# Output stage of a hybrid decoder layer: the samples' product with the weights as the stationary operand

## Chip, cores and metric

The kernel runs on one NeuronCore of a Trainium2 chip. A time is that of one execution on the device, in microseconds. The kernel before was run three times and its median is quoted; one more execution was recorded by the profiler, and all rows come from that one.

## What is computed

One inference step of one decoder layer, for a prompt of 512 positions and for 8 sample sequences of 4 positions each (32 rows). Three token mixers (mLSTM, chunked spatial gating, RG-LRU) share one input projection; their outputs are gated, projected and merged. The change touches only the end:

```python
merged = (jax.nn.sigmoid(g_a) * (y_a @ p['w_proj_a'])
          + jax.nn.sigmoid(g_b) * (y_b @ p['w_proj_b'])
          + jax.nn.sigmoid(g_c) * (y_c @ p['w_proj_c']))
out = merged @ p['w_out']                                    # 1024 x 1024
x_new = layer_norm(ALPHA * x + out, p['ln_g'], p['ln_b'])
```

`x_new` is an output for the prompt's 512 rows (`y_p`) and for the samples' 32 rows (`y_s`), all in float32.

## The kernel before

A matmul on TensorE loads one operand (the stationary one, at most 128x128) and moves the columns of the other past it. Products are made to nearly float32 precision from two parts: each operand is split into a high part (rounded to the type that TensorE multiplies, float32r) and a low part (the rest), and high x high, low x high and high x low are added up in PSUM. The low part's name ends in `l`, the high part's in `h`.

All engines but SyncE run their instructions in the order in which the program writes them. SyncE's DMA issues are ordered by the framework.

`output()` (line 1223) is the last stage. The merged activations lie transposed, features on the partitions: `ms[k]` (k = 0 to 7) is a pair of high and low parts, 128 features x 544 positions, the last 32 of them the samples. `msx` holds the samples alone, for each k 32 high columns and 32 low ones beside each other. The output weights come in two halves of 512 columns; `wos[hf, k]` is the pair of parts of 128 rows x 512 columns. While the first half (`hf` 0) is multiplied, the second half's weights are loaded and split (`wout_half`).

In each half the rows are done in five pieces: four tiles of 128 prompt rows (`i` = 0 to 3) and the samples (`i` = `NCH` = 4). In half 0 the samples come last, in half 1 first (`orders`), so the samples' two products follow each other. A prompt tile takes 24 matmuls: the activations are stationary (128x128), 512 weight columns move. The samples take 16 in each half: 64 columns of `msx` are stationary against the high weights, and 32 against the low ones. The result of the samples' matmuls has high and low rows on different partitions (0 to 31 and 32 to 63), so it is evacuated by VectorE (line 1277), then by ScalarE (line 1283), and added by VectorE (line 1284).

After each piece VectorE adds half of PSUM to the residual `r[i, hf]` (line 1277) and takes the statistics of two times 256 columns (`bn_stats`). In half 1 the norm follows for each piece, here called its finish: `ln_stats` (VectorE, with a reciprocal root on GpSimd, line 1151), half 0's columns on VectorE (`ln_out`, lines 1155 and 1156), half 1's columns on ScalarE and GpSimd (lines 1325 and 1326), an add of VectorE that is put off to the next piece's finish (`late`, line 1331), and two DMAs to the output. The last tile is multiplied in two parts of 256 columns. `rows_in` loads a residual tile and scales it on ScalarE (lines 1244 and 1245), some pieces ahead. PSUM tiles of the kind `aux` (one bank, two buffers) hold the results here; those of the kind `mm` (two banks, two buffers) are the input projections'.

Of the kernel before, what the change touches and what calls it, by code (L numbers as in the profile page):

```python
# [15 lines left out]
P = 128  # L16
D = 1024
KT = 8
# [23 lines left out]
def kernel(  # L42
# [22 lines left out]
    def mm(name):  # L65
        return pm.tile([P, 2, 512], F32, tag="mm", name=name)
# [26 lines left out]
    def matmul(out, a, b, start, stop):  # L93
        cols = math.prod(b.shape[1:])
        clk[0] += cols / 2400 if b.dtype == F32R and cols >= 256 else max(cols, 16) / 600
        PE.matmul(out, a, b, start=start, stop=stop)  # L96
# [1049 lines left out]
    def ln_stats(stt, n, name):  # L1146
        ag = sp.tile([P, 2], F32, tag="bag", name=f"bag{name}", bufs=2)
        V.bn_aggr(ag[:n], stt[:n])
        rs = sp.tile([P, 1], F32, tag="brs", name=f"brs{name}", bufs=2)
        V.tensor_scalar(rs[:n], ag[:n, 1:2], EPS, None, op0=ALU.add)  # L1150
        G.tensor_tensor(rs[:n], rs[:n], mhalf[:n], op=ALU.pow)
        return ag, rs

    def ln_out(out, src, ag, rs, g, b, n):
        V.scalar_tensor_tensor(out, src, ag[:n, 0:1], g[:n, :512], op0=ALU.subtract, op1=ALU.mult)
        V.scalar_tensor_tensor(out, out, rs[:n], b[:n, :512], op0=ALU.mult, op1=ALU.add)
# [66 lines left out]
    def output():  # L1223
        force("wout")
        for c in range(KT - 2, KT):
            ms.append(split(f"ms{c}", mg[c][:, :T], ("x", "x")))

        msx = slot("dm", "msx", F32R)[:, :512].rearrange("p (k c) -> p k c", k=KT)
        for c in range(KT):
            for i in range(2):  # L1230
                G.tensor_copy(msx[:, c, i * NS:(i + 1) * NS], f(ms[c][i][:, SEQ:T]))
        orders = ((0, 1, 2, 3, NCH), (NCH, 0, 1, 2, 3))
        r, stts, late = {}, {}, []
        og, ob = [], []
        nxt = None
        every = [(hf, i) for hf in range(2) for i in orders[hf]]

        def rows_in():
            if len(r) < len(every):
                hf, i = every[len(r)]  # L1240
                n = P if i < NCH else NS
                t_ = slot("dm" if len(r) == 8 else "ya", f"r{i}{hf}")
                src = xpv[i * P:i * P + n] if i < NCH else xsv
                nc.sync.dma_start(t_[:n, :512], src[:, hf * 512:hf * 512 + 512])
                A.activation(t_[:n, :512], t_[:n, :512], AF.Copy, scale=ALPHA)
                r[i, hf] = t_

        rows_in()
        for hf in range(2):
            if hf == 1:  # L1250
                for q in range(2):
                    for dst, src in ((og, ln_g), (ob, ln_b)):
                        a = slot("kv", f"ol{len(dst)}{q}")
                        nc.sync.dma_start(a[:, :512], src[0:1, q * 512:q * 512 + 512].to_broadcast([P, 512]))
                        dst.append(a)
            for oi, i in enumerate(orders[hf]):
                n = P if i < NCH else NS
                rows_ = slice(i * P, i * P + n)
                dst = y_p[0, rows_] if i < NCH else y_s.rearrange("b s d -> (b s) d")
                t_ = r[i, hf]  # L1260

                last = hf == 1 and oi == NCH
                for c0 in range(0, 512, 256) if last else (0,):
                    cw = slice(c0, c0 + 256) if last else slice(0, 512)
                    ps = aux(f"out{i}{hf}{c0}")[:, cw]
                    for k in range(KT):
                        wh_, wl_ = (w_[:, cw] for w_ in wos[hf, k])
                        if i < NCH:
                            for n_, (a, b) in enumerate(((ms[k][0], wh_), (ms[k][1], wh_), (ms[k][0], wl_))):
                                matmul(ps, a[:, rows_], b, start=(k == 0 and n_ == 0), stop=(k == KT - 1 and n_ == 2))  # L1270
                        else:
                            if k:
                                matmul(ps[:NS, :], msx[:, k, 0:NS], wl_, start=False, stop=False)
                            matmul(ps[:2 * NS, :], msx[:, k, :], wh_, start=(k == 0), stop=(k == KT - 1))
                            if k == 0:
                                matmul(ps[:NS, :], msx[:, k, 0:NS], wl_, start=False, stop=False)
                    V.scalar_tensor_tensor(t_[:n, cw], ps[:n, :], 0.5, t_[:n, cw], op0=ALU.mult, op1=ALU.add)
                    if last:
                        V.bn_stats(stts[i][:n, 2 + c0 // 256, :], t_[:n, cw])
                rows_in()  # L1280
                if i == NCH:
                    lo = sp.tile([P, 512], F32, tag="c0l", name=f"outl{hf}", bufs=2)
                    A.activation(lo[:NS, :], ps[NS:2 * NS, :], AF.Copy, scale=0.5)
                    V.tensor_tensor(t_[:NS, :512], t_[:NS, :512], lo[:NS, :], op=ALU.add)
                if hf == 0:
                    for k in (2 * oi, 2 * oi + 1):
                        if k < KT:
                            raw, hi, lo = wout_half(1, k)
                            A.activation(hi[:, :512], raw, AF.Copy)
                            V.tensor_tensor(lo[:, :512], raw, f(hi[:, :512]), op=ALU.subtract)  # L1290
                            wos[1, k] = (hi[:, :512], lo[:, :512])
                    stts[i] = sp.tile([P, 4, 6], F32, tag="bsto", name=f"bsto{i}", bufs=5)
                if not last:
                    for q in range(2):
                        V.bn_stats(stts[i][:n, 2 * hf + q, :], t_[:n, q * 256:q * 256 + 256])
                if hf == 0:
                    continue
                ag, rs = ln_stats(stts[i], n, f"o{i}")
                if not last:
                    for fin in late:  # L1300
                        fin()
                    late.clear()
                t_, ra = r[i, 1][:n, :512], r[i, 0][:n, :512]
                if last:

                    qa, qb = slice(0, 384), slice(384, 512)
                    parts = ((ra, og[0][:n, :512], ob[0][:n, :512]), (t_[:, qa], og[1][:n, qa], ob[1][:n, qa]))
                    for x_, g_, _ in parts:
                        V.scalar_tensor_tensor(x_, x_, ag[:n, 0:1], g_, op0=ALU.subtract, op1=ALU.mult)
                    nm = sp.tile([P, 1], F32, tag="bnm", name=f"bnm{i}", bufs=2)  # L1310
                    V.scalar_tensor_tensor(nm[:n], ag[:n, 0:1], -1.0, rs[:n], op0=ALU.mult, op1=ALU.mult)
                    A.activation(t_[:, qb], t_[:, qb], AF.Identity, bias=nm[:n], scale=rs[:n])
                    G.tensor_tensor(t_[:, qb], t_[:, qb], og[1][:n, qb], op=ALU.mult)
                    G.tensor_tensor(t_[:, qb], t_[:, qb], ob[1][:n, qb], op=ALU.add)
                    for x_, _, b_ in parts:
                        V.scalar_tensor_tensor(x_, x_, rs[:n], b_, op0=ALU.mult, op1=ALU.add)
                        c0 = 0 if x_ is ra else 512
                        nc.sync.dma_start(dst[:, c0:c0 + x_.shape[-1]], x_)
                    for fin in late:
                        fin()  # L1320
                    nc.sync.dma_start(dst[:, 896:1024], t_[:, qb])
                    continue
                nm = sp.tile([P, 1], F32, tag="bnm", name=f"bnm{i}", bufs=2)
                V.scalar_tensor_tensor(nm[:n], ag[:n, 0:1], -1.0, rs[:n], op0=ALU.mult, op1=ALU.mult)
                A.activation(t_, t_, AF.Identity, bias=nm[:n], scale=rs[:n])
                G.tensor_tensor(t_, t_, og[1][:n, :512], op=ALU.mult)
                ln_out(r[i, 0][:n, :512], r[i, 0][:n, :512], ag, rs, og[0], ob[0], n)
                nc.sync.dma_start(dst[:, 0:512], r[i, 0][:n, :512])

                def fin(t_=t_, dst=dst, n=n):  # L1330
                    V.tensor_tensor(t_, t_, ob[1][:n, :512], op=ALU.add)
                    nc.sync.dma_start(dst[:, 512:1024], t_)

                late.append(fin)


    for h in range(H):
# [52 lines left out]
```

## Time and profile before

| | |
|---|---|
| median of 3 runs | 990.83 us (989.39 to 991.03) |
| the profiled execution | 991.64 us |
| its span on the core | 989.9 us |
| TensorE busy | 975.1 us (99% of the span), 7427 matmuls |
| VectorE, ScalarE, GpSimd busy | 56%, 42%, 10% |
| granted TensorE clock, mean | 0.988 of full speed |

The span runs from the first to the last instruction of the core; the execution's time holds 1.7 us more around it. Busy TensorE time counts matmuls that overlap each other in the array, so a matmul's duration is longer than the step from one to the next; steps are read from starts.

### The profile page before, as it was taken

To read this page: it belongs to the slowest core of one execution; us is meant where nothing else is said; L and a number is where in the kernel's file an instruction comes from. 1 tells how busy PE (TensorE), PEld (TensorE's weight loads), DVE (VectorE), ACT (ScalarE), POOL (GpSimd) and SP (SyncE) were. 2 spreads that over 40 slices of the span, in tenths; PEclk is the share of its full clock that TensorE was granted. 3 is DMA by queue.
4 is the path that set the end of the run, shared out by engine and by line. 5 is a ranking of instruction groups with operands and counts; after the bars stand their busy time and mean duration, and the time that the engine had idled before them with its cause. 6 is when DMAs were issued, how large, how long until landed. Compare 5 with 4: busy or idle time off the path is not lost.

```text
span 989.9 us, 17773 instructions
## 1 busy us (share of the span) xinstructions
PE 975.1 (99%) x7427; PEld 950.7 (96%) x7427; DVE 549.6 (56%) x892; ACT 411.2 (42%) x648; POOL 97.3 (10%) x218
## 2 busy tenths in 40 slices
PE   8999999999999999999999999999999999999996
PEld 7999999999999999999999999999999999999975
DVE  3565676566567568889942243333257555433456
ACT  3455446445444544889922232222232313322421
POOL 5121101200210120001000000000000000000204
PEclk7999999999999999999999999999999999999998
DMA  6342723541362253332132222232222313431322
GB/s 209 106 99 91 214 71 98 170 132 62 116 215 67 81 183 95 97 96 92 57 115 85 86 86 85 88 109 90 85 86 96 102 54 107 138 107 44 102 64 101
DMA packets 99392, 103.55 MB, mean 105 GB/s; under 512 B 5342, under 2 KB 91720, under 8 KB 99312
## 3 DMA queue, kind: packets, MB, share of 16 engines
q1 hardware_dynamic: 98416, 102.11, 33.0%
q8 instruction: 58, 0.95, 0.4%
q0 software_dynamic: 896, 0.31, 0.1%
q14 instruction: 22, 0.18, 0.1%
HBM read 90.40 MB, written 12.00 MB: 103 GB/s over the span
## 4 chain that ended last, share of the span: by engine, by line
PE 98%; DMA 1%; ACT 0%; issue 0%; POOL 0%; SPq 0%; DVE 0%; POOLq 0%
PE ps_v L96 5%; PE out L96 5%; PE ps_zc L96 5%; PE ps_u L96 5%; PE ps_z L96 5%; PE ps_q L96 5%; PE ps_vb L96 5%; PE ps_xc L96 5%; PE ps_pa L96 5%; PE ps_zb L96 5%; PE ps_ga L96 5%; PE ps_pc L96 5%; PE ps_o L96 5%; PE ps_k L96 5%; PE ps_gb L96 5%; PE ps_gc L96 5%
## 5 line engine op out<-in xcount | busy, mean ns | idle before, releaser
L798 DVE SCALAR_TENSOR_TENSOR c<-c,bc,cs 128x512 f32<-128x512 f32 x32 | 23.9, 747 | 36.2 <-PE cs L96 35.8
L780 POOL TENSOR_SCALAR wvm<-wvt,bm 96x256 fp32r<-96x256 f32 x32 | 30.4, 951 | 87.9 <-PE cs L96 87.9
L96 PE MATMUL ps_v<-xh,wh_v 128*128 128x272 f32 x128 | 28.6, 304 | 0.6 <-ACT xh L336 0.6
L96 PE MATMUL ps_v<-xl,wh_v 128*128 128x272 f32 x128 | 28.0, 301 | 0.0
L777 ACT ACTIVATE c0h<-c 128x512 fp32r<-128x512 f32 x32 | 20.0, 625 | 18.3 <-DMA c<-in_state_mlstm_c_dram 11.6
L96 PE MATMUL ps_v<-xh,wl_v 128*128 128x272 f32 x128 | 27.5, 298 | 0.0
L96 PE MATMUL ps_q<-xh,wh_q 128*128 128x272 f32 x128 | 27.3, 295 | 0.0
L96 PE MATMUL ps_u<-xh,wh_u 128*128 128x272 f32 x128 | 27.3, 294 | 0.0
L96 PE MATMUL ps_zc<-xl,wh_zc 128*128 128x272 f32 x128 | 27.2, 294 | 0.0
L96 PE MATMUL ps_o<-xl,wh_o 128*128 128x272 f32 x128 | 27.2, 293 | 0.0
L96 PE MATMUL ps_zc<-xh,wl_zc 128*128 128x272 f32 x128 | 27.1, 294 | 0.0
L96 PE MATMUL ps_zc<-xh,wh_zc 128*128 128x272 f32 x128 | 27.1, 293 | 0.0
L96 PE MATMUL ps_z<-xh,wl_z 128*128 128x272 f32 x128 | 26.9, 292 | 0.0
L96 PE MATMUL ps_zb<-xh,wh_zb 128*128 128x272 f32 x128 | 26.9, 291 | 0.0
L96 PE MATMUL ps_o<-xh,wl_o 128*128 128x272 f32 x128 | 26.8, 291 | 0.0
L96 PE MATMUL ps_vb<-xh,wh_vb 128*128 128x272 f32 x128 | 26.8, 290 | 0.0
L96 PE MATMUL ps_q<-xl,wh_q 128*128 128x272 f32 x128 | 26.7, 290 | 0.0
L96 PE MATMUL ps_q<-xh,wl_q 128*128 128x272 f32 x128 | 26.7, 290 | 0.0
L96 PE MATMUL ps_xc<-xl,wh_xc 128*128 128x272 f32 x128 | 26.6, 289 | 0.0
L96 PE MATMUL ps_gc<-xh,wh_gc 128*128 128x272 f32 x128 | 26.6, 289 | 0.0
L96 PE MATMUL ps_gb<-xl,wh_gb 128*128 128x272 f32 x128 | 26.6, 289 | 0.0
L96 PE MATMUL ps_k<-xl,wh_k 128*128 128x272 f32 x128 | 26.6, 289 | 0.0
(776 smaller groups left out, 3282.9 us busy)
## 6 DMA issues: line engine op xcount, KB each, us to landing
c<-in_state_mlstm_c_dram SPq DMA_DIRECT2D x32, 256.0 KB
out_dram<-c SPq DMA_DIRECT2D x32, 256.0 KB
wr_q<-in_w_in_dram SPq DMA_DIRECT2D x8, 512.0 KB
wr_k<-in_w_in_dram SPq DMA_DIRECT2D x8, 512.0 KB
wr_o<-in_w_in_dram SPq DMA_DIRECT2D x8, 512.0 KB
wr_z<-in_w_in_dram SPq DMA_DIRECT2D x8, 512.0 KB
wr_xc<-in_w_in_dram SPq DMA_DIRECT2D x8, 512.0 KB
wr_zc<-in_w_in_dram SPq DMA_DIRECT2D x8, 512.0 KB
```

What stands on the lines that cost most here:

```text
L96: PE.matmul(out, a, b, start=start, stop=stop)
L777: A.activation(hi[:, :512], t_[:, :512], AF.Copy)
L780: G.tensor_scalar(wvm, f(wvs), bm[:, b:b + 1], None, op0=ALU.mult)
L798: V.scalar_tensor_tensor(t_[:, :512], t_[:, :512], inter[:, DS * b + DS - 1:DS * b + DS], ps, op0=ALU.mult, op1=ALU.add)
```

## The change

The samples' product is turned round. In each half, four blocks of 128 weight columns are made stationary one after the other, and the samples' columns of `msx` move: 64 columns against the high weights, 32 against the low ones, for each of the eight k. The result is transposed, weight columns on the partitions, in an `mm` tile. Nothing is done with it at once. After tile 0 of half 1, `sample_rows` adds the high and low columns (ScalarE, then VectorE, into a 128x128 tile `lo`), turns each block back with a transpose on TensorE into the tile's second bank, adds that to the residual and takes the statistics; first for half 0, then for half 1. Then the samples' finish follows, and then tile 0's. The finish itself becomes a function, `finish(i, last)`, with the same instructions as before.

```diff
@@ -1245,6 +1245,76 @@
+        xps = {}
+
+        def sample_products(hf):
+            xps[hf] = ps = mm(f"outs{hf}")
+            for c in range(4):
+                cw = slice(c * P, (c + 1) * P)
+                for k in range(KT):
+                    wh_, wl_ = (w_[:, cw] for w_ in wos[hf, k])
+                    if k:
+                        matmul(ps[:, 0, c * 64:c * 64 + NS], wl_, msx[:, k, 0:NS], start=False, stop=False)
+                    matmul(ps[:, 0, c * 64:c * 64 + 64], wh_, msx[:, k, :], start=(k == 0), stop=(k == KT - 1))
+                    if k == 0:
+                        matmul(ps[:, 0, c * 64:c * 64 + NS], wl_, msx[:, k, 0:NS], start=False, stop=False)
+
+        def sample_rows(hf):
+            ps, t_ = xps[hf], r[NCH, hf]
+            o2 = ps[:, 0, 0:256].rearrange("p (c r s) -> p c r s", c=4, r=2)
+            lo = sp.tile([P, 512], F32, tag="c0l", name=f"outl{hf}", bufs=2)[:, 0:4 * NS]
+            lo4 = lo.rearrange("p (c s) -> p c s", c=4)
+            A.activation(lo4, o2[:, :, 1, :], AF.Copy, scale=0.5)
+            V.scalar_tensor_tensor(lo4, o2[:, :, 0, :], 0.5, lo4, op0=ALU.mult, op1=ALU.add)
+            for c in range(4):
+                transpose(ps[:NS, 1, c * P:(c + 1) * P], lo[:, c * NS:(c + 1) * NS], ident)
+            V.tensor_tensor(t_[:NS, :512], t_[:NS, :512], ps[:NS, 1, :], op=ALU.add)
+            for q in range(2):
+                V.bn_stats(stts[NCH][:NS, 2 * hf + q, :], t_[:NS, q * 256:q * 256 + 256])
...
+        def finish(i, last=False):
...
@@ -1258,30 +1328,21 @@
                 rows_ = slice(i * P, i * P + n)
                 dst = y_p[0, rows_] if i < NCH else y_s.rearrange("b s d -> (b s) d")
                 t_ = r[i, hf]
+                if i == NCH:
+                    sample_products(hf)
 
                 last = hf == 1 and oi == NCH
-                for c0 in range(0, 512, 256) if last else (0,):
+                for c0 in range(0, 512, 256) if last else (0,) if i < NCH else ():
                     cw = slice(c0, c0 + 256) if last else slice(0, 512)
                     ps = aux(f"out{i}{hf}{c0}")[:, cw]
                     for k in range(KT):
                         wh_, wl_ = (w_[:, cw] for w_ in wos[hf, k])
-                        if i < NCH:
-                            for n_, (a, b) in enumerate(((ms[k][0], wh_), (ms[k][1], wh_), (ms[k][0], wl_))):
-                                matmul(ps, a[:, rows_], b, start=(k == 0 and n_ == 0), stop=(k == KT - 1 and n_ == 2))
-                        else:
-                            if k:
-                                matmul(ps[:NS, :], msx[:, k, 0:NS], wl_, start=False, stop=False)
-                            matmul(ps[:2 * NS, :], msx[:, k, :], wh_, start=(k == 0), stop=(k == KT - 1))
-                            if k == 0:
-                                matmul(ps[:NS, :], msx[:, k, 0:NS], wl_, start=False, stop=False)
+                        for n_, (a, b) in enumerate(((ms[k][0], wh_), (ms[k][1], wh_), (ms[k][0], wl_))):
+                            matmul(ps, a[:, rows_], b, start=(k == 0 and n_ == 0), stop=(k == KT - 1 and n_ == 2))
                     V.scalar_tensor_tensor(t_[:n, cw], ps[:n, :], 0.5, t_[:n, cw], op0=ALU.mult, op1=ALU.add)
                     if last:
                         V.bn_stats(stts[i][:n, 2 + c0 // 256, :], t_[:n, cw])
                 rows_in()
-                if i == NCH:
-                    lo = sp.tile([P, 512], F32, tag="c0l", name=f"outl{hf}", bufs=2)
-                    A.activation(lo[:NS, :], ps[NS:2 * NS, :], AF.Copy, scale=0.5)
-                    V.tensor_tensor(t_[:NS, :512], t_[:NS, :512], lo[:NS, :], op=ALU.add)
                 if hf == 0:
                     for k in (2 * oi, 2 * oi + 1):
                         if k < KT:
@@ -1290,48 +1351,19 @@
                             V.tensor_tensor(lo[:, :512], raw, f(hi[:, :512]), op=ALU.subtract)
                             wos[1, k] = (hi[:, :512], lo[:, :512])
                     stts[i] = sp.tile([P, 4, 6], F32, tag="bsto", name=f"bsto{i}", bufs=5)
+                if i == NCH:
+                    continue
                 if not last:
                     for q in range(2):
                         V.bn_stats(stts[i][:n, 2 * hf + q, :], t_[:n, q * 256:q * 256 + 256])
                 if hf == 0:
                     continue
-                ag, rs = ln_stats(stts[i], n, f"o{i}")
...
-                late.append(fin)
+                if oi == 1:
+
+                    for q in range(2):
+                        sample_rows(q)
+                    finish(NCH)
+                finish(i, last)
```

## Rows read from the trace of the kernel before

**Rows 1.** The page, part 4: shares of the chain that ended last, by engine.
```profile
PE 98%; DMA 1%; ACT 0%; issue 0%; POOL 0%; SPq 0%; DVE 0%; POOLq 0%
```

**Rows 2.** Timeline, 950.5 to 965.5 us: start, duration, engine, line, operation, out<-in.
```profile
951.41 0.40 PE L96 MATMUL out<-wol,ms7h 128*128 128x512 f32 x1
...
951.65 0.39 PE L96 MATMUL out<-woh,msx 128*64 128x512 f32 x1
...
951.85 0.69 DVE L1277 SCALAR_TENSOR_TENSOR r<-out,r 128x512 f32<-128x512 f32 x1 [3.00 <-PE out L96]
...
959.04 0.40 PE L96 MATMUL out<-woh,ms0h 128*128 128x512 f32 x1
...
964.39 0.39 PE L96 MATMUL out<-wol,ms7h 128*128 128x512 f32 x1
```

**Rows 3.** Timeline of VectorE in the second half of the output stage.
```profile
962.06 0.25 DVE L1148 BATCH_NORM_AGGREGATE bago<-bsto 32x2 f32<-32x24 f32 x1
...
964.82 0.69 DVE L1277 SCALAR_TENSOR_TENSOR r<-out,r 128x512 f32<-128x512 f32 x1
...
965.54 0.75 DVE L1295 BATCH_NORM_STATS2 bsto<-r 128x6 f32<-128x256 f32 x2
...
966.33 0.26 DVE L1148 BATCH_NORM_AGGREGATE bago<-bsto 128x2 f32<-128x24 f32 x1
...
968.70 0.75 DVE L1156 SCALAR_TENSOR_TENSOR r<-r,brso,ol 128x512 f32<-128x512 f32 x1
...
976.10 0.69 DVE L1277 SCALAR_TENSOR_TENSOR r<-out,r 128x512 f32<-128x512 f32 x1 [0.98 <-PE out L96]
...
980.63 0.42 DVE L1277 SCALAR_TENSOR_TENSOR r<-out,r 128x256 f32<-128x256 f32 x1
...
981.76 0.42 DVE L1277 SCALAR_TENSOR_TENSOR r<-out,r 128x256 f32<-128x256 f32 x1 [0.25 <-PE out L96]
```

**Rows 4.** Timeline of TensorE, three stretches with short matmuls or transposes, merged.
```profile
37.24 1.10 PE L96 MATMUL fps<-sels,gsb 128*128 128x4 f32 x10
...
761.39 1.04 PE L100 MATMUL vt<-ident,vbt 128*32 128x128 f32 x8
...
29.64 0.68 PE L100 MATMUL sps<-ident,cvh 32*128 32x32 f32 x8
```

**Rows 5.** Views of three tiles: instructions, duration in ns (least, median, most), starts, shapes.
```profile
L96 PE MATMUL fps<-sels,gsb x10: 169/252/253, 37.2 to 38.2; 128*128 128x4 f32 x8, 128*32 128x4 f32 x2
...
L100 PE MATMUL vt<-ident,vbt x40: 269/272/274, 721.7 to 762.2; 128*128 128x128 f32 x32, 128*32 128x128 f32 x8
...
L100 PE MATMUL sps<-ident,cvh x8: 222/222/243, 29.6 to 30.1; 32*128 32x32 f32 x8
...
L867 DVE SCALAR_TENSOR_TENSOR u<-to,sps x8: 179/181/189, 118.1 to 376.0; 128x32 f32<-128x32 f32 x8
```

**Rows 6.** Timeline of GpSimd, second half of the output stage.
```profile
964.29 1.67 POOL L1326 TENSOR_TENSOR r<-r,ol 32x512 f32<-32x512 f32 x1 [1.11 <-ACT r L1325]
...
966.93 0.88 POOL L1151 TENSOR_TENSOR brso<-brso,mhalf 128x1 f32<-128x1 f32 x1 [0.97 <-DVE brso L1150]
```

**Rows 7.** Stretches: length, busy time of each engine, TensorE's granted clock (PEclk), DMA share.
```profile
6.00:8.00 2.00, 0.66 (x4) 0.42 (x4) 0.00 (x0) 0.00 (x0) 0.82 (x1) 1.00 1.09 280
...
8.00:10.00 2.00, 1.80 (x8) 1.57 (x8) 0.00 (x0) 0.23 (x1) 1.30 (x3) 0.50 1.06 369
...
18.00:20.00 2.00, 2.00 (x17) 2.00 (x16) 0.69 (x1) 0.88 (x2) 0.65 (x2) 0.94 0.02 8
...
959.00:981.60 22.60, 22.60 (x121) 19.23 (x119) 16.93 (x38) 5.41 (x8) 9.57 (x8) 1.00 0.19 66
...
984.00:985.00 1.00, 0.00 (x0) 0.00 (x0) 1.00 (x4) 0.49 (x1) 0.19 (x1) 0.61 0.00 0
```

**Rows 8.** Timeline of TensorE in the first 22 us.
```profile
15.14 3.42 PE L100 MATMUL xps<-ident,x 128*128 128x128 f32 x16
```

**Rows 9.** Timeline of SyncE's DMA issues, second half of the output stage.
```profile
966.47 0.33 SPq L1244 DMA_DIRECT2D r<-in_x_prompt_dram  x1
```

More of the change, by code (lines that the diff above doesn't have):

```diff
@@ new lines, in finish, with fin @@
+        def finish(i, last=False):
+            n = P if i < NCH else NS
+            dst = y_p[0, i * P:i * P + n] if i < NCH else y_s.rearrange("b s d -> (b s) d")
+            ag, rs = ln_stats(stts[i], n, f"o{i}")
+            if not last:
+                for fin in late:
+                    fin()
+                late.clear()
+            t_, ra = r[i, 1][:n, :512], r[i, 0][:n, :512]
+            if last:
+                qa, qb = slice(0, 384), slice(384, 512)
+                parts = ((ra, og[0][:n, :512], ob[0][:n, :512]), (t_[:, qa], og[1][:n, qa], ob[1][:n, qa]))
+                for x_, g_, _ in parts:
+                    V.scalar_tensor_tensor(x_, x_, ag[:n, 0:1], g_, op0=ALU.subtract, op1=ALU.mult)
+                nm = sp.tile([P, 1], F32, tag="bnm", name=f"bnm{i}", bufs=2)
+                V.scalar_tensor_tensor(nm[:n], ag[:n, 0:1], -1.0, rs[:n], op0=ALU.mult, op1=ALU.mult)
+                A.activation(t_[:, qb], t_[:, qb], AF.Identity, bias=nm[:n], scale=rs[:n])
+                G.tensor_tensor(t_[:, qb], t_[:, qb], og[1][:n, qb], op=ALU.mult)
+                G.tensor_tensor(t_[:, qb], t_[:, qb], ob[1][:n, qb], op=ALU.add)
+                for x_, _, b_ in parts:
+                    V.scalar_tensor_tensor(x_, x_, rs[:n], b_, op0=ALU.mult, op1=ALU.add)
+                    c0 = 0 if x_ is ra else 512
+                    nc.sync.dma_start(dst[:, c0:c0 + x_.shape[-1]], x_)
+                for fin in late:
+                    fin()
+                nc.sync.dma_start(dst[:, 896:1024], t_[:, qb])
+                return
+            nm = sp.tile([P, 1], F32, tag="bnm", name=f"bnm{i}", bufs=2)
+            V.scalar_tensor_tensor(nm[:n], ag[:n, 0:1], -1.0, rs[:n], op0=ALU.mult, op1=ALU.mult)
+            A.activation(t_, t_, AF.Identity, bias=nm[:n], scale=rs[:n])
+            G.tensor_tensor(t_, t_, og[1][:n, :512], op=ALU.mult)
+            ln_out(r[i, 0][:n, :512], r[i, 0][:n, :512], ag, rs, og[0], ob[0], n)
+            nc.sync.dma_start(dst[:, 0:512], r[i, 0][:n, :512])
+            def fin(t_=t_, dst=dst, n=n):
+                V.tensor_tensor(t_, t_, ob[1][:n, :512], op=ALU.add)
+                nc.sync.dma_start(dst[:, 512:1024], t_)
+            late.append(fin)
@@ L1297, in output @@
                     continue
-                ag, rs = ln_stats(stts[i], n, f"o{i}")
[L1299 to L1332, printed above, removed]
```

## Prediction

> **What bounds the kernel now.** I read the page's chain of waits first: 98% of it is TensorE [rows 1]. So a microsecond added to TensorE's queue anywhere before the end, as work or as waiting, is a microsecond of the result, while VectorE, ScalarE, GpSimd and the DMA queues cost something only where TensorE, or the last tile's chain, waits for them. The second view is the timeline of the output stage. The samples' products run there twice, back to back: the first begins at 951.65 and the first matmul of tile 0 of the second half follows at 959.04 [rows 2]. That is 7.39 us for 32 matmuls of 512 columns, 0.231 us apiece, and TensorE never pauses in it. VectorE's own timeline is the third view. With tile 3 of the second half it becomes the one that ends last: it takes the first 256 columns of that tile's result at 980.63 and the second at 981.76 [rows 3]; from there the end is a chain of small steps which the change leaves alone.
>
> The change therefore has two places to look at: the products themselves, and the point behind tile 0 of the second half, where the samples' rows are now turned back.
>
> **Products.** Removed: 32 matmuls that load 64 or 32 columns of samples and move 512 columns of weights, 7.39 us. Added: in each half 4 x 8 pairs, 128 matmuls in all, which load 128 columns of weights each and move 64 or 32. Nothing of this shape is in the trace, so it is bounded by short matmuls that are. Ten matmuls that load mostly 128x128 and move only 4 columns cover 1.10 us; less the last one's own 0.17 to 0.25, nine steps take 0.85 to 0.93, 0.10 us each [rows 4, 5]. With 4 columns there is next to nothing to move, so I read this as the pace of the load. Eight transposes that move 128 columns cover 1.04 us, of which the last is 0.27: seven steps of 0.11 [rows 4, 5]. The fastest row of short work is eight transposes of 32 partitions with 32 moving columns: (0.68 - 0.22) / 7 = 0.066 us [rows 4, 5]. The new loads fill all 128 partitions and are no transposes, so they are nearest to the first row. The kernel's own planner (line 95) books 64 columns of this type at 0.107 us and 32 at 0.053, that is, it takes moving fewer than 256 columns as four times as dear per column. I take 0.11 for the 64-column matmul and 0.10, the load's pace, for the 32-column one: 64 x 0.21 = 13.4 us, so **+6.1 us**. The ends: 128 x 0.066 = 8.4, +1.1; 128 x 0.11 = 14.1, +6.7; and at the lower clock far more (a rival, below).
>
> The Trainium skill, "TensorE: Matmul & The Clock Gate", section on the back-to-back issue gap, gives pairs of a load and a matmul of 128 columns a sustained 81 ns. By that, as an estimate, the products would take 128 x 0.081 = 10.4 us and cost 3.0 more than now instead of 6.1; the rows of this trace for loads of 128 columns are slower, so they decide.
>
> **Turning the rows back.** After tile 0's matmuls TensorE's queue now holds four transposes for half 0, four for half 1, and behind them tile 1's matmuls. Each four wait for a 128x128 tile that VectorE writes, and VectorE works its list in the order in which it is written: tile 0's result, its two statistics, half 0's sum, then the add of the transposed rows and two statistics, and only then half 1's sum. So tile 1 waits for all that. Time runs from the start of tile 0's last matmul (964.39 in the trace, rows 2):
> - VectorE takes a tile's result 0.44 after its last matmul began (951.41 to 951.85) [rows 2]; from there 0.72 and 0.79 go for the result and the statistics (964.82, 965.54, 966.33) [rows 3]. So 1.95.
> - Half 0's sum, 128x128 from PSUM, lies between 0.18 (128x32) [rows 5] and 0.42 us (128x256, at 980.63) [rows 3]; I take 0.28, 2.23. The ScalarE copy it needs has no late input and is done while tile 0 is multiplied.
> - Four transposes: a load and three steps of 0.11, the last one's 0.27, two hand-overs of some 0.05: the add begins at 3.05.
> - Add and statistics as above, 1.51: 4.56. Half 1's sum: 4.84. Then the load and four transposes: tile 1 begins at 5.44 and not at 0.23. **TensorE is 5.2 us late**, of which the eight transposes are 0.9 and two idle stretches of about 2 us the rest.
> - VectorE goes on: the second add at 5.66, with its statistics until 7.17; the samples' finish takes 2.76 (962.06 to 964.82) [rows 3], 9.93. Then tile 0's finish, whose root on GpSimd queues behind the samples' multiply there. That multiply began 2.23 after the finish did (964.29) and takes 1.67 [rows 6], so it ends at 11.07; from the root's start (966.93) [rows 6] to the end of the finish (968.70 + 0.75) [rows 3] are 2.52: 13.6.
> - Then VectorE is behind and does tiles 1 and 2 one after the other, 4.53 each (976.10 to 980.63) [rows 3]: 22.66. The first part of tile 3 takes 0.45 and as much for its statistics: the second part is taken at 23.6. Before it was 981.76 - 964.39 = 17.4. So **+6.2 us** if nothing else is late; TensorE's own delay would make it 5.2.
>
> **The clock.** The granted clock is 1.00 (2.4 GHz) through the second half of the output stage [rows 7], but the trace shows when it falls. At the end it fell in the stretch 984 to 985 (mean 0.61) [rows 7], after VectorE had taken the last matmul's result at 981.76 [rows 3]. At the start it was 1.00 from 6 to 8 us with TensorE busy 0.66 of 2.00 us, and 0.50 (1.2 GHz) from 8 on; it came back at about 18, in the stretch with 0.94 [rows 7], after 16 transposes on end had taken 3.42 us, 0.2 apiece [rows 8], against 0.11 later [rows 4, 5]. Two idle stretches of 2 us with half a microsecond of transposes between them are emptier than what went ahead of the fall at 8 us. I hold a fall here for likelier than not. Tile 1 would then be multiplied in part at twice 0.23 per matmul; between half and all of its 5.5 us at the low clock loses 1.5 to 3 us of TensorE. Of that 1.1 us is hidden, since VectorE is behind by that much (23.6 against 17.4 + 5.2). TensorE then ends 6.7 to 8.2 late; I take **+7.4** for the place.
>
> The same page of the Trainium skill, in the section on loop structure, warns of idle gaps between bursts of matmuls, after which the clock is at half rate; it speaks against this change, and the fall near 984 agrees with it.
>
> **What I cost at nothing.** The samples' two evacuations at the half boundary go away: VectorE does them while TensorE is busy with tile 0, so nothing is gained. The norm's gains and offsets are loaded as the first half's weights come free, some 7 us later than now, because the new loop reads all eight weight tiles until its last block; they are first used by the samples' finish, 20 us on. The load of the last residual tile waits for the samples' first half to be written out (966.47 now) [rows 9]; it comes some 9 us later and lands by about 14 on the clock above, used at 22.7: 8 us of cover. Accumulators of the projections are reused, long free.
>
> **Sum.** 6.1 + 7.4 = 13.5 us. The profiled execution took 991.64, 0.81 over the median of 990.83; 1005.1 there, **1004.3** as a median.
>
> **Rivals.**
> - The clock holds: 6.1 + 6.2 = 12.3, 1003.1. For it: each idle stretch alone is shorter than the time from the last matmul to the fall near 984.
> - The loads go at 0.066: 1.1 + 7.4 = 8.5, 999.3. For it: nothing but that faster row; against: its 32 partitions.
> - The clock falls within the products, which move few columns for 13 us on end. Short matmuls would go at 0.20; half of them so is 19.2 us, all of them 25.6: with the 6.2 to 7.4 behind, +18 to +26, 1009 to 1016. Against it: the rise near 18 us came in a run of transposes.
> - No wait behind tile 0, should the samples' rows be ready ahead of tile 0's result: only the eight transposes, 6.1 + 0.9 = 7.0, 997.8. Against: before, every engine kept the written order.
> - Not slower: loads are hidden whole and only moved columns count, 0.231 / 512 per column: 64 x 96 columns are 2.8 us, 4.6 less than now. With +6.2 behind, +1.6, inside what a measurement of this kernel tells from no change (0.2%, 2.0 us). It decides below 7.39 - 6.2 + 2.0 = 3.2 us of products, 0.025 per matmul; the 0.10 of the row with 4 columns speaks against it.
>
> **Chances.** Forecast 0.52; clock holds 0.20; faster loads 0.10; low clock in the products 0.10; no wait 0.04; loads hidden 0.03; hidden and without the wait, thus faster, 0.01. The range of 998.5 to 1008.5 takes in the first three with their bounds, 0.82. Faster 0.01, same 0.03, slower 0.96.
>
> **What would show it.** The new matmuls at 0.10 to 0.11 apiece, 13 to 14 us between tile 3 of half 0 and tile 0 of half 1; two gaps of about 2 us on TensorE behind tile 0, ended by VectorE; a granted clock below 1.00 in tile 1; VectorE without idle time from there on. Wrong would be: gaps under 1 us, a pace under 0.08, or a clock at 0.50 among the products.

## Result and profile after

The changed kernel takes 1014.15 us (median of 6 runs, 1009.87 to 1015.71) against 989.89 for the kernel before (6 runs): a ratio of 1.0237, 95% interval 1.0219 to 1.0254. It is 24 us slower. I had forecast slower, by 13.5 us, and the range ended at 1008.5.

The profiled execution, 1009.87 us with a span of 1008.2, is the shortest of the six. It reached the output stage 5.7 us earlier than the one before (first prompt matmul of half 0 at 923.74 against 929.41), although the code ahead of that stage is the same: the granted clock reads 1.00 over its first 20 us, where that of before had 0.74, and the 16 transposes that took 3.42 us there [rows 8] took 1.91 here. The row is that of the first 20 us: length, busy time of TensorE, its loads, VectorE, ScalarE and GpSimd, the granted clock, DMA share and rate.

```profile
0.00:20.00 20.00, 16.10 (x110) 14.20 (x111) 8.56 (x22) 9.13 (x22) 14.10 (x34) 1.00 0.82 258
```

At the start of an execution the granted clock has to be read together with the steps between starts. In the first kernel of the experiments it reads 1.00 from 0 to 20 us too, yet the same 16 transposes took 3.52 us there, about as long as at 0.50. In the output stage the clock and the steps agree in every run below.

The stage began between 923.74 and 929.71 us in the eight profiled executions of this document. So stages are compared with stages here, from the samples' first matmul on. From there to the end of the span the kernel before takes 989.9 - 951.65 = 38.25 us and the changed one 1008.2 - 945.97 = 62.2: 24.0 more, the whole of the difference of the medians.

The page's shares of the chain still give TensorE nearly everything, a little less than in [rows 1]:

```profile
PE 97%; DVE 1%; DMA 1%; ACT 0%; issue 0%; SPq 0%; POOL 0%; POOLq 0%; DVEq 0%
```

The timeline of TensorE in the changed kernel (start, duration, operation; in brackets the idle time ahead and what ended it) answers to [rows 2]:

```profile
945.97 0.19 PE L96 MATMUL outs<-msx,woh 128*128 128x64 f32 x1
...
946.33 0.26 PE L96 MATMUL outs<-msx,wol 128*128 128x32 f32 x1
946.44 0.28 PE L96 MATMUL outs<-msx,woh 128*128 128x64 f32 x1
...
951.85 0.40 PE L96 MATMUL outs<-msx,woh 128*128 128x64 f32 x1
952.06 0.37 PE L96 MATMUL outs<-msx,wol 128*128 128x32 f32 x1
...
968.06 0.40 PE L96 MATMUL outs<-msx,woh 128*128 128x64 f32 x1
968.27 0.77 PE L96 MATMUL out<-woh,ms0h 128*128 128x512 f32 x1
...
971.81 0.40 PE L96 MATMUL out<-wol,ms2h 128*128 128x512 f32 x1
...
975.31 0.40 PE L96 MATMUL out<-wol,ms7h 128*128 128x512 f32 x1
977.54 0.61 PE L100 MATMUL outs<-ident,outl 128*32 128x128 f32 x4 [1.83 <-DVE outl L1270]
979.88 1.03 PE L100 MATMUL outs<-ident,outl 128*32 128x128 f32 x4 [1.74 <-DVE outl L1270]
980.57 0.78 PE L96 MATMUL out<-woh,ms0h 128*128 128x512 f32 x1
```

The samples' matmuls start 0.11 us apart at first (946.33, 946.44) and 0.21 apart from about 951 on (951.85, 952.06). They end at 968.27, 22.3 us after they began. Tile 0 starts 0.43 apart and is normal again from 971.81. Behind it are the two waits, of 1.83 and 1.74 us, ended by VectorE's sums, and tile 1 begins 5.26 us after tile 0's last matmul and not 0.23 after it.

The granted clock in stretches of the same execution (columns as above) answers to [rows 7]:

```profile
951.00:953.00 2.00, 2.00 (x13) 2.00 (x12) 0.00 (x0) 0.00 (x0) 0.00 (x0) 0.57 0.07 28
...
965.00:967.00 2.00, 2.00 (x12) 2.00 (x11) 0.00 (x0) 0.00 (x0) 0.00 (x0) 0.50 0.00 0
971.00:973.00 2.00, 2.00 (x9) 1.61 (x8) 0.00 (x0) 0.00 (x0) 0.00 (x0) 0.81 0.00 0
975.00:977.00 2.00, 0.71 (x4) 0.22 (x2) 1.15 (x3) 0.00 (x0) 0.00 (x0) 1.00 0.00 0
977.00:979.00 2.00, 0.61 (x4) 0.31 (x4) 1.26 (x4) 0.00 (x0) 0.00 (x0) 0.90 0.00 0
979.00:981.00 2.00, 1.11 (x5) 0.93 (x6) 0.87 (x4) 0.00 (x0) 0.00 (x0) 0.50 0.00 0
...
987.00:989.00 2.00, 2.00 (x10) 1.59 (x10) 1.87 (x5) 1.34 (x2) 0.97 (x1) 1.00 0.13 33
```

Two falls are to be seen. The first is at about 951, within the samples' products, with TensorE busy 2.00 of 2.00 us; the clock is back at about 972. The second is at about 979, in the waits. VectorE's timeline answers to [rows 3]:

```profile
975.81 0.69 DVE L1342 SCALAR_TENSOR_TENSOR r<-out,r 128x512 f32<-128x512 f32 x1 [27.09 <-PE out L96]
...
977.21 0.27 DVE L1270 SCALAR_TENSOR_TENSOR outl<-outs,outl 128x128 f32<-128x128 f32 x1
978.19 0.68 DVE L1273 TENSOR_TENSOR r<-r,outs 32x512 f32<-32x512 f32 x1 [0.70 <-PE outs L100]
...
979.57 0.26 DVE L1270 SCALAR_TENSOR_TENSOR outl<-outs,outl 128x128 f32<-128x128 f32 x1
980.96 0.68 DVE L1273 TENSOR_TENSOR r<-r,outs 32x512 f32<-32x512 f32 x1 [1.13 <-PE outs L100]
...
999.99 0.42 DVE L1342 SCALAR_TENSOR_TENSOR r<-out,r 128x256 f32<-128x256 f32 x1 [0.24 <-PE out L96]
```

VectorE's order is as written: tile 0's result, half 0's sum, its add, half 1's sum, its add. From 975.31, the start of tile 0's last matmul, to 999.99, where the second part of tile 3 is taken, are 24.7 us; before they were 17.4.

The 24.0 us by stage: products 22.3 - 7.4 = 14.9; tile 0, in its first half at the low clock, (975.31 - 968.27) - (964.39 - 959.04) = 1.7; the place behind tile 0, 24.7 - 17.4 = 7.3; the end, 0.1.

### The profile page after: what moved, and what is told of

It reads as the page before. It is cut to its first block, busy times and chain, and to the rows that moved or that the text cites. A ratio compares the mean times of both kernels' runs of the same rounds, so it can differ in the third digit from the quotient of the medians.

```text
span 1008.2 us, 17982 instructions
## 1 busy us (share of the span) xinstructions
PE 990.5 (98%) x7531; PEld 967.6 (96%) x7531; DVE 548.5 (54%) x892; ACT 410.7 (41%) x648; POOL 96.9 (10%) x218
## 4 chain that ended last, share of the span: by engine, by line
PE 97%; DVE 1%; DMA 1%; ACT 0%; issue 0%; SPq 0%; POOL 0%; POOLq 0%; DVEq 0%
PE ps_zc L96 5%; PE ps_u L96 5%; PE ps_z L96 5%; PE ps_q L96 5%; PE ps_v L96 5%; PE out L96 5%; PE ps_vb L96 5%; PE ps_xc L96 5%; PE ps_pa L96 5%; PE ps_zb L96 5%; PE ps_ga L96 5%; PE ps_pc L96 5%; PE ps_o L96 5%; PE ps_k L96 5%; PE ps_gc L96 5%; PE ps_gb L96 5%
## 5 line engine op out<-in xcount | busy, mean ns | idle before, releaser
L1342 DVE SCALAR_TENSOR_TENSOR r<-out,r 128x512 f32<-128x512 f32 (+1 forms) x9 | 5.7, 632 | 40.0 <-PE out L96 39.9
```

## Experiments

Two costs are in dispute, and both of them with the clock: why it fell in the products, and what the wait behind tile 0 costs with and without it. The first four kernels ran beside one series of the kernel before (median 988.37 us, 7 runs), the last two beside another (989.02, 11 runs). Stage times are those from the samples' first matmul to the end of the span, 38.25 in the kernel before.

**1. The rows turned back early, the products as changed.** `sample_rows` is cut into three, `sums` (ScalarE and VectorE), `turns` (the four transposes) and `adds` (VectorE).

```diff
                 if i == NCH:
                     sample_products(hf)
+                    if hf == 1:
+                        sums(0)
+                        turns(0)
+                        adds(0)
+                        sums(1)
...
+                        if hf == 1 and i == 0 and k == 2:
+                            turns(1)
+                            adds(1)
+                            finish(NCH)
...
-                if oi == 1:
-
-                    for q in range(2):
-                        sample_rows(q)
-                    finish(NCH)
                 finish(i, last)
```

> Only the place where the samples' rows are turned back is changed: both halves' sums on VectorE and ScalarE come before tile 0's result, half 0's transposes follow the products, half 1's stand after three of eight k of tile 0, the samples' finish comes before tile 0's again. The products are those of the change. Theory (the wait behind tile 0 cost 7.3 us, the low clock in the products is a matter of its own): no gaps on TensorE, clock at 0.50 in the products as before, about +17 to +18 us over the kernel before, 6 to 7 under the change. Rival (the two gaps drag the clock down for the whole stage, products included): products back at 0.11 us apiece, about +8.

Measured: 1007.54 us, ratio 1.0184 (1.0159 to 1.0208), 19.2 over before. The stage takes 1006.4 - 950.67 = 55.7 us, 17.5 more than before. The products are one piece of 22.3 us in the chain of waits in order of time (start, length, what):

```profile
950.83 22.33 PE outs L96 x128
```

and the granted clock by stretches is

```profile
951.00:954.00 3.00, 3.00 (x29) 3.00 (x28) 2.42 (x5) 0.00 (x0) 0.00 (x0) 1.00 0.00 0
954.00:957.00 3.00, 3.00 (x25) 3.00 (x24) 0.00 (x0) 0.00 (x0) 0.00 (x0) 0.83 0.02 5
957.00:960.00 3.00, 3.00 (x16) 3.00 (x16) 0.14 (x1) 0.28 (x1) 0.00 (x0) 0.50 0.74 216
...
978.00:981.00 3.00, 3.00 (x14) 2.42 (x13) 2.18 (x7) 0.42 (x1) 0.54 (x1) 1.00 0.00 0
```

The clock falls at about 956, with TensorE busy without a gap since the products began and no wait before it, and is back at about 976.5. So the products lower it by themselves, and the rival, that the gaps drag it down, is out. Turning the rows back early saves 62.2 - 55.7 = 6.5 us.

**2. Four copies of the columns, 256 moved.** The same 128 matmuls and loads. The results fill two banks, so each half's sum is made in two steps.

```diff
-                    wh_, wl_ = (w_[:, cw] for w_ in wos[hf, k])
-                    if k:
-                        matmul(ps[:, 0, c * 64:c * 64 + NS], wl_, msx[:, k, 0:NS], start=False, stop=False)
-                    matmul(ps[:, 0, c * 64:c * 64 + 64], wh_, msx[:, k, :], start=(k == 0), stop=(k == KT - 1))
...
+                    moving = msx[:, k:k + 1, :].to_broadcast([P, 4, 64])
+                    for n_, w_ in enumerate(wos[hf, k]):
+                        matmul(o, w_[:, cw], moving, start=(k == 0 and n_ == 0), stop=(k == KT - 1 and n_ == 1))
```

> As the change, but each of the 128 sample matmuls moves 256 columns, four copies of the 64, instead of 64 or 32 (the low weights meet the low columns too, a term that the change leaves out). Loads and their number are the same. Theory (the clock falls because few columns are moved): clock 1.00 through the products, 0.12 us apiece, 15 us in place of 22, tile 0 at the full clock; about +15 us over the kernel before, so 8 to 9 less than the change for three to eight times the columns. Rival (the clock falls because of 128 different loads in a row): 0.23 apiece, 29 us, about +31.

Measured: 1004.56 us, ratio 1.0158 (1.0136 to 1.0180), 16.2 over before. The stage takes 1005.1 - 951.94 = 53.2 us, 14.9 more than before and 9.1 less than the change. The step in TensorE's timeline:

```profile
951.94 0.28 PE L96 MATMUL outs<-msx,woh 128*128 128x256 f32 x1
952.06 0.28 PE L96 MATMUL outs<-msx,wol 128*128 128x256 f32 x1
```

and the stretches:

```profile
960.00:963.00 3.00, 3.00 (x27) 3.00 (x27) 0.00 (x0) 0.00 (x0) 0.00 (x0) 1.00 0.80 279
972.00:975.00 3.00, 0.81 (x4) 0.33 (x2) 1.75 (x5) 0.34 (x2) 0.00 (x0) 1.00 0.00 0
...
978.00:981.00 3.00, 3.00 (x10) 2.34 (x10) 1.81 (x5) 0.00 (x0) 0.00 (x0) 0.50 0.02 5
```

Steps of 0.12 us at a clock of 1.00 through all the products. Moving four and eight times the columns past the same loads makes the products 7 us shorter. The clock falls again in the wait behind tile 0 (972 to 978), as in the change; with the sums in two steps the two gaps are 2.28 and 2.18 us long here.

**3. Two copies, 128 columns.** The diff is the same with 2 in place of 4, and the results fit one bank again.

> As the one before with two copies, 128 columns (again with the low-by-low term). It tells what a column costs in matmuls under 256 columns. If it costs what it does in long ones, the load sets the pace, 0.11 us apiece at the full clock and 0.21 at the low one: +14 if the clock holds, +24 if it falls as in the change. If it costs four times as much, as the kernel's planner books it, 128 columns take 0.21 us at the full clock, 28 us of products, and the array always moves, so that the clock holds: about +28.

Measured: 1002.36 us, ratio 1.0131 (1.0111 to 1.0151), 14.0 over before; the stage takes 1000.2 - 949.73 = 50.5 us, 12.2 more than before. TensorE's timeline, two of the products and the wait:

```profile
949.90 0.27 PE L96 MATMUL outs<-msx,woh 128*128 128x128 f32 x1
950.01 0.28 PE L96 MATMUL outs<-msx,wol 128*128 128x128 f32 x1
...
969.38 0.40 PE L96 MATMUL out<-wol,ms7h 128*128 128x512 f32 x1
971.60 0.61 PE L100 MATMUL outs<-ident,outl 128*32 128x128 f32 x4 [1.83 <-DVE outl L1272]
973.95 0.61 PE L100 MATMUL outs<-ident,outl 128*32 128x128 f32 x4 [1.73 <-DVE outl L1272]
974.32 0.47 PE L96 MATMUL out<-woh,ms0h 128*128 128x512 f32 x1
```

and the stretches:

```profile
960.00:963.00 3.00, 3.00 (x29) 3.00 (x28) 0.00 (x0) 0.00 (x0) 0.00 (x0) 1.00 0.03 10
969.00:972.00 3.00, 1.17 (x8) 0.59 (x6) 1.63 (x4) 0.00 (x0) 0.00 (x0) 1.00 0.00 0
972.00:975.00 3.00, 1.27 (x9) 0.93 (x8) 2.01 (x5) 0.00 (x0) 0.00 (x0) 1.00 0.00 0
```

0.11 us for 128 columns, just what the change's 64 and 32 cost at the full clock. So up to 128 the moved columns do not set the pace; the load, of 128 columns in each case, is what is left. The fourfold price per column that the kernel's planner books under 256 columns (line 95) is not what was measured: for 128 columns it would be 0.21. The clock is 1.00 in the products, and in this kernel the wait did not lower it either, though the two gaps are as long as those of the change (1.83 and 1.73 us).

**4. The change's short matmuls in portions of 16.** Half 0's blocks follow prompt tiles 0 to 3, half 1's stand inside tile 0.

```diff
+                        if hf == 0 and k == KT - 1:
+                            sample_block(0, i)
+                        if hf == 1 and i == 0 and k % 2 == 1:
+                            sample_block(1, k // 2)
+                            if k == KT - 1:
+                                sums(1)
```

> The change's short matmuls, but never more than 16 in a row: half 0's four blocks one after each prompt tile of half 0, half 1's four inside tile 0 of half 1, after every six of its matmuls; rows turned back without a wait, half 1's a tile later. Theory (a long run of them lowers the clock): granted clock 1.00 throughout, 0.11 us apiece, 14 us of products, about +8 us over the kernel before. Rival (any of them does): clock below 1.00 among them and +12 or more.

Measured: 1002.47 us, ratio 1.0131 (1.0107 to 1.0154), 14.1 over before, where 8 was expected. From the first prompt matmul of half 0 the stage takes 12.3 us more than before (72.8 against 60.5). The timeline and the stretches show what I had overlooked:

```profile
959.61 0.28 DVE L1272 SCALAR_TENSOR_TENSOR outl<-outs,outl 128x128 f32<-128x128 f32 x1
...
959.94 0.86 PE L100 MATMUL outs<-ident,outl 128*32 128x128 f32 x4 [1.13 <-DVE outl L1272]
```

```profile
940.00:945.00 5.00, 5.00 (x32) 4.38 (x31) 2.56 (x5) 1.15 (x2) 0.00 (x0) 1.00 0.04 14
...
960.00:963.00 3.00, 3.00 (x10) 2.43 (x11) 1.42 (x3) 0.00 (x0) 0.00 (x0) 0.53 0.63 208
963.00:966.00 3.00, 3.00 (x21) 2.78 (x21) 0.00 (x0) 0.00 (x0) 0.00 (x0) 0.90 0.00 0
```

Among the portions of half 0 the clock is 1.00 (one of them lies in the first stretch shown; from 929 to 960 us it never falls). But half 0's transposes stand at the head of half 1 and wait 1.13 us for VectorE, straight after a portion of short matmuls; the clock falls there, and tile 0 begins at 0.50. The run says that the portions of half 0 did not lower the clock by themselves, and is spoiled as a price.

**5. Both costs undone: early rows, 128 columns.** The edits of the first and the third.

> Both suspected costs undone at once: rows turned back early as in the first run, 128 columns moved as in the third (with the low-by-low term). Theory (load pace, low clock and wait are all there is): products 128 x 0.111 = 14.2 us, 6.8 over the 7.4 of before, 0.9 for eight transposes, clock 1.00 throughout, no gap: +7.7 us over the kernel before, and 6 to 7 under the third run, which is the wait behind tile 0 with the clock held. Rival (the wait's cost moves to VectorE, which must then do the samples' work beside tile 0 and ends late): +10 or more.

Measured: 996.45 us, ratio 1.0079 (1.0064 to 1.0094), 7.4 over before. The stage takes 997.0 - 951.03 = 46.0 us, 7.7 more than before, as expected to the tenth. The stretches hold the products, tile 0 and the rest:

```profile
950.00:965.00 15.00, 15.00 (x132) 14.77 (x131) 2.85 (x6) 0.28 (x1) 0.00 (x0) 1.00 0.22 71
965.00:971.00 6.00, 6.00 (x33) 4.94 (x33) 3.42 (x9) 0.80 (x2) 0.51 (x1) 1.00 0.00 0
971.00:988.00 17.00, 17.00 (x95) 14.68 (x94) 13.76 (x31) 4.83 (x7) 8.35 (x8) 1.00 0.26 87
```

TensorE is busy all the time at a clock of 1.00. Against the third kernel the stage is 50.5 - 46.0 = 4.5 us shorter: that is the wait behind tile 0 with the clock held, less the eight transposes, which both have.

**6. The portions again, without the wait.** Half 0's transposes move into tile 0.

```diff
                     if hf == 1:
                         sums(0)
-                        turns(0)
-                        adds(0)
...
+                        if hf == 1 and i == 0 and k == 4:
+                            turns(0)
+                            adds(0)
```

> As the fourth run, but half 0's transposes stand after five of eight k of tile 0 and not ahead of it, where they waited 1.1 us for VectorE. The matmuls move 64 and 32 columns again, at most 16 in a row. Theory (long runs of short matmuls, or short ones beside a gap, lower the clock): clock 1.00 from 930 us to the last matmul, 14 us of products, +8 us, the same as with 128 columns within a microsecond or so. Rival (few columns lower the clock however they lie): a stretch below 1.00 in tile 0 of half 1, where they are densest, and +10 or more.

Measured: 1000.49 us, ratio 1.0108 (1.0092 to 1.0123), 11.5 over before; its stage, counted as in the fourth, takes 70.0 us, 9.5 more. The stretches of half 0, and of the products of half 1:

```profile
930.00:957.00 27.00, 27.00 (x146) 22.89 (x144) 9.88 (x19) 8.39 (x15) 1.06 (x3) 1.00 0.19 60
957.00:972.00 15.00, 15.00 (x108) 13.74 (x108) 3.98 (x9) 1.09 (x4) 0.00 (x0) 1.00 0.23 70
```

The clock is 1.00 with 64 and 32 columns, in tile 0 of half 1 too, where the portions are densest. So the rival, that few columns lower it however they lie, is out. The price missed, and 1.4 us of the miss are on VectorE:

```profile
969.57 0.40 PE L96 MATMUL out<-wol,ms7h 128*128 128x512 f32 x1
...
972.23 0.68 DVE L1363 SCALAR_TENSOR_TENSOR r<-out,r 128x512 f32<-128x512 f32 x1
...
990.83 0.41 DVE L1363 SCALAR_TENSOR_TENSOR r<-out,r 128x256 f32<-128x256 f32 x1
```

I had put half 1's sum, which waits for the last portion, ahead of tile 0's result, which is taken 2.66 us after that tile's last matmul began and not 0.44 [rows 2]. VectorE never caught up: the last part of tile 3 is taken 1.76 us after the last matmul (begun at 989.07), against 0.33 before (981.43 to 981.76). Then 6.8 for the products, 0.9 for the transposes and 1.4 for this are 9.1 of the stage's 9.5 us. By the medians about 2 us more are open. They are open in the first four kernels too, whose medians lie 1.7, 1.3, 1.8 and 1.8 us further above the kernel before than their stages do; in the fifth it is 0.3 less. The time ahead of the output stage differs by more than that from one profiled execution to the next, so it may lie there; no run shows it.

No version of the turned product beat the kernel before. Even with both faults mended it is 7.4 us slower.

## Why the prediction was wrong

**The step that failed is the products' clock.** I took the upper level as given there and made the fall a rival, with a chance of 0.10 and 1009 to 1016 us; the medians came out inside that rival. Against it I had put that the clock rose at the start of the kernel in a run of transposes. That row does not bear on it: those transposes move 128 columns for each load, as the third kernel does, in which the clock held too. The change moves 64 and 32. I had the short rows of the trace at 1.00, but each lasted about a microsecond or less [rows 4], and the change puts 128 such matmuls in a row. The fourth and the sixth kernel show that in portions of 16 between long matmuls they leave the clock alone. The fall is not that of one execution: the mean granted clock of all six of the change lies between 0.979 and 0.982 and of the four of the first kernel between 0.978 and 0.983, while those of the kernel before that ran beside the experiments, and of the second to sixth kernels, lie between 0.988 and 0.996. The low clock took 22.3 - 14.2 = 8.1 us of the products and 1.7 of tile 0, 9.8 of the 10.5 us by which the stage's 24.0 passed the 13.5 of the sum.

**The pace** was 0.11 for both kinds and not 0.11 and 0.10; 14.2 us and not 13.4. The row with 4 columns gave it nearly; the 81 ns of the Trainium skill ("TensorE: Matmul & The Clock Gate", section on the back-to-back issue gap) is not borne out here, at 111 ns measured for these float32r matmuls. With the planner's price I came out right by chance: 64 columns at its fourfold rate are 0.107, but 128 are not 0.21.

**The place behind tile 0** was forecast at 7.4 us and came out at 7.3. TensorE was 5.0 us late (5.2 forecast), the sums took 0.27 (0.28), tile 1 ran in part at the low clock and took 980.57 to 988.45, 7.9 us in place of 24 x 0.232 = 5.6, 2.3 lost (1.5 to 3). That it was the clock and not VectorE that ended last there is seen in the changed kernel at 999.99, where VectorE waits 0.24 us for TensorE. With the clock held (third kernel) the place costs 992.04 - 969.38 = 22.7 against 17.4, 5.3 and not the 6.2 of the step list, which booked tile 0's root on GpSimd at 0.88 where it took 0.54, and the adds' start some tenths late.

**The idle stretches** were followed by a fall in the change (1.83 and 1.74 us) and in the second kernel (2.28 and 2.18), not in the third (1.83 and 1.73, the gaps of the change). So "likelier than not" is all that these runs bear out; what decides it was not separated. The page of the Trainium skill that I cited beside it ("TensorE: Matmul & The Clock Gate"), in its section on loop structure, speaks of long waits between matmuls. The falls of the change and of the second kernel in their gaps go with it, the third kernel's holding does not, and the first kernel's fall without any gap is not covered by it.

**Costs at nothing** held: gains and offsets, the last residual tile and the accumulators held nobody up. All sits on TensorE, as [rows 1] said it would.

What stays open: whether it is the columns of the 64-wide or of the 32-wide matmuls that let the clock fall, since no kernel here ran one kind alone; whether it is only their number, since the second and third kernels move copies of the same columns and add the low-by-low term; and the last 2 us of the sixth.

## What to carry to other kernels

Before operands are swapped, count the loads: 32 matmuls that move 512 columns at 0.231 us are cheaper than 128 that move few at 0.11, since each of those loads 128 columns and none here went faster. Where a change puts a long run of matmuls with fewer moving columns than any run in the trace, both levels of the clock are likely cases, and TensorE's busy time, which is full in either, does not tell them apart; read the granted clock, and check it against the steps between starts. And put a transpose into TensorE's queue only behind work that outlasts the engine that writes its input: here that was worth 4.5 us with the clock held and 6.5 as changed.

## What was unexpected in the hardware

- TensorE, busy without a gap, fell from 2.4 to 1.2 GHz while it moved 64 and 32 columns per load (1.00 to 0.50 at about 951 in the changed kernel, which began these matmuls at 945.97, and at about 956 in the first, which began them at 950.67). With 128 or 256 columns it stayed at 2.4 GHz through all 128 matmuls, 14 and 15 us.
- A matmul of this type that loads 128 columns and moves 128 costs 0.11 us, no more than one that moves 32: moved columns were free up to there.
- A gap of 1.13 us behind 16 short matmuls was followed by a fall (0.53 in the stretch after it), two gaps of 1.8 us behind long matmuls once were not.
- The granted clock can read 1.00 at the start of an execution while TensorE goes at half pace: 16 transposes took 3.52 us in the first kernel at 1.00, and 3.42 in the kernel before at 0.50 [rows 8].
